# Both FFN products of a streaming-encoder layer by seven half-size products

## The chip, the cores and the metric

The kernel runs on one core of a Trainium2 chip. The metric is device time in microseconds, the median of several runs of the whole program. TensorE is written PE, VectorE DVE, ScalarE ACT, GpSimd POOL, SyncE SP; SP issues most transfers.

## The reference

One layer of a streaming encoder over 2048 prompt tokens and 64 sample tokens, 2112 in all, width 1024, in float32. Attention and a causal depthwise convolution feed an output projection; then come the FFN, a gated embedding and a final norm. What matters here is this:

```python
    mixed = jnp.concatenate([rms_norm(attn, lp['attn_out_g']), rms_norm(conv, lp['conv_out_g'])], axis=-1)
    x = x + mixed @ lp['w_out']
    f = rms_norm(x, lp['norm_ffn_g']) @ lp['w_ff_up']              # 1024 -> 4096
    x = x + jnp.square(jax.nn.relu(f)) @ lp['w_ff_down']           # 4096 -> 1024
    x = x + jax.nn.sigmoid(rms_norm(x, lp['norm_ple_g']) @ lp['w_ple_gate']) * (p @ lp['w_ple_proj'])
```

## The kernel before

The tokens stand in 17 tiles of 128 (the last has 64). Up to three tiles make a piece, two pieces a block, and there are three blocks (line 53), of 768, 640 and 704 tokens. Phase 1 projects the input, phase 2 is attention, phase 3 (`phase3`) takes the blocks one after the other through output projection, FFN, gated embedding and final norm.

Every float32 product is made of three matmuls, `mm3` (lines 177 to 181): both operands are split into a rounded high part (a cast on ACT) and the rest (a difference, on DVE unless another engine is named) by `split` (lines 163 to 165), and high by high, high by low and low by high are added up in PSUM.

The FFN walks through the 4096 hidden channels in eight chunks of four slices of 128. For each slice `up` (line 973) multiplies the 1024 x 128 weights with each of the two pieces, 24 matmuls over as many columns as the piece has tokens; ACT and DVE take max(0, x) squared from PSUM to SBUF, and the result is split. Then the down product multiplies the four slices with their 1024 columns of down weights; each token tile and half of the output has 12 matmuls of 512 columns, and DVE adds the bank to the tile's row of `x1` (lines 1058 to 1061). The last piece, whose tokens end in half a tile, is multiplied with the weights as the stationary operand instead and transposed at the end (`down_tall`, line 997). Nothing of the FFN leaves SBUF. The norm of the FFN's input is not applied to its operand: since relu squared is homogeneous, its square is multiplied in where the down product is added (`Y`, line 1060).

The operand of the up product is made by `operand` (lines 202 to 219), eight groups of transposes with their split: for one piece as soon as its output projection is done, while PE projects the other. In the same way `prepare` and `mixed` (lines 838 to 861) make the operand of the next block's output projection during the gate of the present one, in SBUF tiles of their own (`h`, three of them), so that loads of the next block do not wait for rows of this one.

Matmuls go round four PSUM banks (`mm`), transposes round three (`tr`), one bank is left to the convolution. The convolution of later pieces, 31 taps per channel and token on DVE in small steps, is background work: `pin` (line 167) queues so many steps behind an instruction of the FFN. A scheduler orders the instructions of each engine beforehand; on the chip each engine takes them in that order. It looks at priorities and free buffers, and the number of buffers of a name (`bufs`) says how far a producer can run ahead.

## Time and profile before

| | |
|---|---|
| median of three runs | 3080.7 us (3079.17 to 3084.36) |
| span of the profiled execution | 3076.4 us |
| PE busy | 2940.3 us, 96% |
| PE weight loads busy | 2604.4 us, 85% |
| DVE busy | 2047.9 us, 67% |
| ACT busy | 1215.2 us, 40% |
| POOL busy | 878.3 us, 29% |

The span goes from the first instruction to the last. The profiled execution's time is this span and what little lies around it; the median of the runs is 4.3 us above the span. Busy is the time in which an engine has an instruction under way. Matmuls are pipelined, so PE counts as busy even where the next matmul could have started earlier, and how fast it works is read from the distance between starts. Phase 3 begins at about 1130 us and takes the rest of the span.

### The profile page before, as it was taken

Reading aid. Unit: us, or ns where it says so; the run is one execution under the profiler, and the core shown is the slowest. Engines: PE = TensorE matmul, PEld = TensorE weight load, DVE = VectorE, ACT = ScalarE, POOL = GpSimd, SP = SyncE. Lnnn points to the kernel's source line nnn. Section 1 sums busy time; section 2 is a strip of 40 time slices with the busy share of each in tenths; the row PEclk is TensorE's granted clock in tenths of the full one; section 3 lists DMA queues with packets and bytes.
Section 4 is the critical chain, followed back from the end, with each engine's and each line's share of the span. In section 5 each row is a group of like instructions: output and inputs, shape, how many; then the busy total and the mean of one; then the engine's idle time right before and its main releaser. Section 6 shows DMA issues by size and latency. Waiting matters only on the chain.

```text
span 3076.4 us, 42553 instructions
## 1 busy us (share of the span) xinstructions
PE 2940.3 (96%) x15586; PEld 2604.4 (85%) x15586; DVE 2047.9 (67%) x3533; ACT 1215.2 (40%) x2404; POOL 878.3 (29%) x1498
## 2 busy tenths in 40 slices
PE   8998899989989879999999999999999999999998
PEld 7997888667667769999999888998998799999986
DVE  4489693999999866666665556787775544444453
ACT  6443342767666734222222433222234432321242
POOL 3235555877776730002002020003022100000001
PEclk9999999999998989999999999999999999999999
DMA  6635258743331132111222242232232411221121
GB/s 200 207 115 181 82 167 166 107 66 57 56 53 31 32 123 74 61 57 64 71 84 78 81 162 69 68 108 68 73 109 92 144 48 62 83 76 55 62 92 45
DMA packets 148601, 279.12 MB, mean 91 GB/s; under 512 B 38136, under 2 KB 78824, under 8 KB 146952
## 3 DMA queue, kind: packets, MB, share of 16 engines
q1 hardware_dynamic: 123800, 244.35, 24.7%
q0 software_dynamic: 24592, 32.06, 6.5%
q8 instruction: 122, 2.00, 0.3%
q14 instruction: 87, 0.71, 0.1%
HBM read 225.67 MB, written 51.28 MB: 90 GB/s over the span
## 4 chain that ended last, share of the span: by engine, by line
PE 72%; DVE 15%; DMA 4%; issue 4%; POOL 3%; ACT 1%; SPq 1%; DVEq 0%; POOLq 0%; ACTq 0%
PE mm L179 23%; PE mm L181 23%; PE mm L180 23%; DVE pl L754 6%; DVE mx L715 3%; DVE cacc L614 2%; PE tr L211 2%; PE tr L714 1%; PE acc L762 1%; DMA qr<-q_s 1%; DMA qr<-in_mq 1%; DMA h<-in_x 1%; POOL rt L153 0%; POOL ry L155 0%; DVE su L777 0%
## 5 line engine op out<-in xcount | busy, mean ns | idle before, releaser
L179 PE MATMUL mm<-thi,uh 128*128 128x384 f32 (+2 forms) x1488 | 480.8, 324 | 0.0
L180 PE MATMUL mm<-tlo,uh 128*128 128x384 f32 (+2 forms) x1488 | 480.7, 323 | 0.0
L181 PE MATMUL mm<-thi,ul 128*128 128x384 f32 (+2 forms) x1488 | 480.3, 323 | 0.0
L614 DVE SCALAR_TENSOR_TENSOR cacc<-cu,cw,cacc 128x384 f32<-128x384 f32 (+2 forms) x720 | 445.1, 632 | 7.3
L758 POOL TENSOR_TENSOR px<-px 128x512 f32<-128x512 f32 (+5 forms) x304 | 399.6, 1315 | 124.7 <-ACT px L753 65.4
L179 PE MATMUL mm<-wdh,ah 128*128 128x512 f32 x896 | 349.5, 391 | 4.9 <-DVE x L1060 2.9
L180 PE MATMUL mm<-wdl,ah 128*128 128x512 f32 x896 | 348.8, 390 | 0.0
L181 PE MATMUL mm<-wdh,al 128*128 128x512 f32 x896 | 345.2, 390 | 0.0
L983 ACT ACTIVATE rl<-mm 128x384 f32<-128x384 f32 (+1 forms) x192 | 88.1, 459 | 590.6 <-PE mm L181 590.2
L152 POOL TENSOR_TENSOR rt<-ry 128x3 f32<-128x3 f32 (+2 forms) x150 | 38.0, 254 | 987.0 <-DVE ry L149 980.2
L754 DVE TENSOR_TENSOR pl<-px,ph 128x512 fp32r<-128x512 f32 (+5 forms) x344 | 309.3, 913 | 15.2 <-ACT px L753 14.1
L1060 DVE SCALAR_TENSOR_TENSOR x<-mm,y,x 128x512 f32<-128x512 f32 x224 | 166.6, 749 | 206.9 <-PE mm L181 204.8
L180 PEld LDWEIGHTS mm<-tlo,uh 128*128 128x128 f32 x1488 | 280.2, 188 | 0.5
L179 PEld LDWEIGHTS mm<-thi,uh 128*128 128x128 f32 x1488 | 279.9, 188 | 0.7
L181 PEld LDWEIGHTS mm<-thi,ul 128*128 128x128 f32 x1488 | 280.1, 188 | 0.1
L165 DVE TENSOR_TENSOR wdl<-raw,wdh 128x1024 fp32r<-128x1024 f32 x139 | 170.8, 1230 | 116.7 <-ACT wdh L164 115.5
L752 ACT ACTIVATE ph<-mm 128x512 fp32r<-128x512 f32 (+5 forms) x344 | 179.3, 522 | 119.6 <-PE mm L181 102.4
L164 ACT CAST wdh<-raw 128x1024 fp32r<-128x1024 f32 x139 | 146.0, 1050 | 157.9 <-DMA raw<-in_wdn 87.1
L179 PEld LDWEIGHTS mm<-wdh,ah 128*128 128x128 f32 x896 | 168.3, 188 | 40.6 <-DVE x L1060 3.3
L181 PEld LDWEIGHTS mm<-wdh,al 128*128 128x128 f32 x896 | 168.2, 188 | 35.0
L180 PEld LDWEIGHTS mm<-wdl,ah 128*128 128x128 f32 x896 | 168.3, 188 | 33.7
L602 POOL DMA_DIRECT2D cu<-u_s x20 | 11.2, 558 | 637.9 <-DVE cacc L614 637.5
(297 smaller groups left out, 6854.4 us busy)
## 6 DMA issues: line engine op xcount, KB each, us to landing
raw<-in_wup SPq DMA_DIRECT2D x96, 512.0 KB, 3.2
raw<-in_wdn SPq DMA_DIRECT2D x96, 512.0 KB, 3.2
raw<-in_wglu SPq DMA_DIRECT2D x24, 512.0 KB, 4.6
raw<-in_wout SPq DMA_DIRECT2D x24, 512.0 KB, 4.5
raw<-in_wgate SPq DMA_DIRECT2D x24, 512.0 KB, 3.8
v_s<-vst SPq DMA_DIRECT2D x36, 256.0 KB, 2.8
v<-v_s POOLq DMA_DIRECT2D x8, 1152.0 KB, 9.2
h<-in_x SPq DMA_DIRECT2D x16, 512.0 KB, 4.5
```

Of the source, the lines that this page charges most:

```text
L164: self.nc.scalar.copy(out=hi, in_=raw)
L165: return (eng or self.nc.vector).tensor_tensor(out=lo, in0=raw, in1=hi.bitcast(F32), op=ALU.subtract)
L179: t.matmul(ps, sh, mh, start=start, stop=False)
L180: t.matmul(ps, sh, ml, start=False, stop=False)
L181: t.matmul(ps, sl, mh, start=False, stop=stop)
L614: nc.vector.scalar_tensor_tensor(out=a, in0=U[:, k:k + W], scalar=w, in1=a, op0=ALU.mult, op1=ALU.add)
L715: nc.vector.tensor_reduce(out=mx[:n, b:b + 1] if nb > 1 else top, in_=ps[:n, :w], axis=AX.X, op=ALU.max, negate=True)
L752: nc.scalar.activation(out=ph[b:, s], in_=ps[:, s], func=AF.Exp)
L754: nc.vector.tensor_tensor(out=pl[b:, s], in0=px[b:, s], in1=ph[b:, s].bitcast(F32), op=ALU.subtract)
L758: nc.gpsimd.tensor_tensor(out=rs[b:, s], in0=rs[b:, s], in1=px[b:, s], op=ALU.add)
L983: nc.scalar.activation(out=rl[:, :N], in_=ps[:, :N], func=AF.Relu)
L1060: r = nc.vector.scalar_tensor_tensor(out=x1[t][:n, cs], in0=ps[:n, :], scalar=Y[q][:n, j:j + 1], in1=x1[t][:n, cs], op0=ALU.mult, op1=ALU.add)
```

## The change

Both products of the FFN are made by one level of Strassen's multiplication in Winograd's form: each operand is cut into four quarters, seven products of quarters replace eight, and sums of quarters are formed before and after. Quarters of the weights are halves of the 4096 hidden channels by halves of the 1024 model channels, quarters of the activations are halves of the model (or hidden) channels by halves of a block's tokens. For this the blocks become 768, 768 and 576 tokens, halves of 384, 384 and 288; in the last block a half ends inside the tile of sample tokens.

- **Up operands.** When both pieces of a block are projected, `x1` is normalised, stored to DRAM (`x_s`) and scaled in place; transposed quarters go to `xf`, POOL forms four sums of them per group of channels (`winograd_right`), and seven operands `X[1]` to `X[7]` are split, in the SBUF that held the operands and weights of the output projection.
- **Up product**, 16 steps j of two slices of 128 hidden channels each. POOL forms four sums of the weight quarters (`winograd`); the seven weight quarters are split; each product has 12 matmuls. The order is 1, 2, 6, 5, 7, 4, 3; products 1, 6, 7 and 4 add up in one bank, 5 and 3 in another after 2 has left it, and in between ACT copies the bank's present content, so that each output is a copy plus a bank. Then relu squared, and POOL forms four sums of the four results; seven quarters of 128 x N are written to DRAM (`a_s`).
- In block 0 each step also forms four sums of the down weights on POOL and writes them to DRAM (`wt_s`), for all blocks.
- **Down product**, seven products of 16 steps: an activation quarter (192 KB, or 144 KB) and a 128 x 512 weight quarter (256 KB) are loaded and split (the activation's low part on POOL, the weight's on DVE), then nine matmuls of 512 columns into three banks (in the last block twelve of 288 into four); after each product the banks are added to one or two output quarters in `x1`, which is loaded again from DRAM.
- **Around it.** Rows of `x1`, the raw weights of the up product and the `h` of the next block now share six buffers (`x4`); `prepare` and `mixed` for the next block come behind `final` of the piece. Convolution steps are pinned two to an up step and two to five down steps.

The diff, cut to its core:

```diff
-BLOCKS = [[[0, 1, 2], [3, 4, 5]], [[6, 7, 8], [9, 10]], [[11, 12, 13], [14, 15, 16]]]
+BLOCKS = [[[0, 1, 2], [3, 4, 5]], [[6, 7, 8], [9, 10, 11]], [[12, 13], [14, 15, 16]]]
+PROD = [1, 2, 6, 5, 7, 3, 4]
...
+    def winograd(self, eng, x11, x12, x21, x22, new):
+        s1, s2, s3, s4 = new(), new(), new(), new()
+        eng.tensor_tensor(out=s1, in0=x21, in1=x22, op=ALU.add)
+        eng.tensor_tensor(out=s2, in0=s1, in1=x11, op=ALU.subtract)
+        eng.tensor_tensor(out=s3, in0=x11, in1=x21, op=ALU.subtract)
+        eng.tensor_tensor(out=s4, in0=x12, in1=s2, op=ALU.subtract)
+        return {1: x11, 2: x12, 3: s4, 4: x22, 5: s1, 6: s2, 7: s3}
+    def winograd_right(self, eng, x11, x12, x21, x22, new):
+        t1, t2, t3, t4 = new(), new(), new(), new()
+        eng.tensor_tensor(out=t1, in0=x12, in1=x11, op=ALU.subtract)
+        eng.tensor_tensor(out=t2, in0=x22, in1=t1, op=ALU.subtract)
+        eng.tensor_tensor(out=t3, in0=x22, in1=x12, op=ALU.subtract)
+        eng.tensor_tensor(out=t4, in0=x21, in1=t2, op=ALU.subtract)
+        return {1: x11, 2: x21, 3: x22, 4: t4, 5: t1, 6: t2, 7: t3}
...
+            def x4(name="x1"):
+                return pc_.tile([P, D], F32, name=name, tag="x1", bufs=6)
+            def r2(name="raw"):
+                return pc_.tile([P, 512], F32, name=name, tag="r2", bufs=6)
+            def w2():
+                return pc_.tile([P, 512], F32R, name="wh", bufs=10), pc_.tile([P, 512], F32R, name="wl", bufs=10)
+            def a15(dt=F32, name="a"):
+                return pc_.tile([P, 384], dt, name=name, tag="a15", bufs=13)
...
             def prepare(pi):
-                hs = [p.tile([P, D], F32, name="h", bufs=3) for _ in self.pieces[pi].tiles]
+                hs = [x4("h") for _ in self.pieces[pi].tiles]
...
+                        y = self.norms([x1[t] for t in pc.tiles], pc.tiles)
+                        for j, t in enumerate(pc.tiles):
+                            n = TILES[t][1]
+                            nc.sync.dma_start(out=x_s[t], in_=x1[t][:n, :])
+                            nc.vector.tensor_scalar(out=x1[t][:n, :], in0=x1[t][:n, :], scalar1=y[:n, j:j + 1],
+                                                    scalar2=None, op0=ALU.mult)
...
+                for k in range(4):
+                    a, b = left[k]
+                    c_, d_ = quad(k, 1), quad(k + 4, 1)
+                    T = self.winograd_right(nc.gpsimd, a, c_, b, d_, lambda: a15(name="xt")[:, :N])
+                    for i in (6, 5, 7, 3, 4):
+                        into(i, k, T[i])
...
+                for j in range(NJ):
+                    ra, rb = x4("ru"), x4("ru")
+                    nc.sync.dma_start(out=ra.rearrange("p (k c) -> p k c", k=KD), in_=I["wup"][j])
+                    nc.sync.dma_start(out=rb.rearrange("p (k c) -> p k c", k=KD), in_=I["wup"][j + NJ])
+                    S = self.winograd(nc.gpsimd, ra[:, :512], ra[:, 512:], rb[:, :512], rb[:, 512:], lambda: r2("s"))
...
+                    product(1, px, True)
+                    nc.scalar.copy(out=y11, in_=px[:, :N])
+                    product(2, py, True)
+                    nc.vector.tensor_tensor(out=y11, in0=py[:, :N], in1=y11, op=ALU.add)
+                    square(y11)
+                    product(6, px, False)
+                    nc.scalar.copy(out=y12, in_=px[:, :N])
+                    product(5, py, True)
+                    product(7, px, False)
+                    nc.scalar.copy(out=y22, in_=px[:, :N])
+                    nc.vector.tensor_tensor(out=y22, in0=py[:, :N], in1=y22, op=ALU.add)
+                    square(y22)
+                    product(4, px, False)
+                    nc.scalar.activation(out=y21, in_=px[:, :N], func=AF.Relu)
+                    product(3, py, False)
+                    nc.vector.tensor_tensor(out=y12, in0=py[:, :N], in1=y12, op=ALU.add)
+                    r = square(y12)
+                    A = self.winograd(nc.gpsimd, y11, y21, y12, y22, lambda: a15(name="as")[:, :N])
+                    for i in PROD:
+                        nc.sync.dma_start(out=a_s[i, j], in_=A[i])
...
+                    for j in range(NJ):
+                        ar = a15()[:, :N]
+                        nc.sync.dma_start(out=ar, in_=a_s[i, j])
+                        ah, al = a15(F32R, "ah")[:, :N], a15(F32R, "al")[:, :N]
+                        r = self.split(ar, ah, al, nc.gpsimd)
+                        wr = r2()
+                        if i in raw_of:
+                            f, h = raw_of[i]
+                            nc.sync.dma_start(out=wr, in_=I["wdn"][(f + j) * P:(f + j + 1) * P, h * 512:(h + 1) * 512])
+                        else:
+                            nc.sync.dma_start(out=wr, in_=wt_s[i, j])
+                        wh, wl = w2()
+                        r = self.split(wr, wh, wl)
+                        for b in range(nb):
+                            cs = slice(b * P, (b + 1) * P)
+                            if tall:
+                                self.mm3s(ps[b][:, :N], wh[:, cs], wl[:, cs], ah, al, fresh and j == 0, j == NJ - 1)
+                            else:
+                                self.mm3s(ps[b], ah[:, cs], al[:, cs], wh, wl, fresh and j == 0, j == NJ - 1)
...
                     if h == 1 and (bi < 2 or q == 0):
                         final(pc.tiles, x1, gfin)
+                    if h == 1 and bi < 2:
+                        M1 = mixed(2 * bi + 2 + q, prepare(2 * bi + 2 + q))
```

Where the change moves instructions, three places of the queues show it.

PE in the up product of block 0: before, at the border of two pieces (`mm` are PSUM banks, `uh`, `ul`, `wdh`, `wdl` weights, `thi`, `tlo` the operand).

```order
L181 MATMUL mm_13905<-thi_13654,wdl_13870 128x384
L179 MATMUL mm_13905<-thi_13654,wdh_13869 128x384
L180 MATMUL mm_13905<-tlo_13655,wdh_13869 128x384
L181 MATMUL mm_13905<-thi_13654,wdl_13870 128x384
L179 MATMUL mm_13951<-thi0_13499,uh_13945 128x384
L180 MATMUL mm_13951<-tlo0_13500,uh_13945 128x384
```

The same engine after, at the border of products 7 and 4 of a step (`T12`, `T13` are operand 7, `T6`, `T7` operand 4).

```order
L904 MATMUL mm_14240<-T13_13746,wh_14313 128x384
L905 MATMUL mm_14240<-T12_13745,wl_14314 128x384
L903 MATMUL mm_14240<-T6_13739,wh_14333 128x384
L904 MATMUL mm_14240<-T7_13740,wh_14333 128x384
L905 MATMUL mm_14240<-T6_13739,wl_14334 128x384
```

Before, the next 24 matmuls go to another bank; after, both products write the same bank, and the copy of the bank stands between them on ACT.

POOL ahead of block 0's FFN: before, the end of a norm, its square and the loads of the convolution.

```order
L154 TENSOR_SCALAR rt_13713<-rt_13713 128x3
L155 TENSOR_TENSOR ry_13712<-ry_13712,rt_13713 128x3
L969 TENSOR_TENSOR y2_13729<-ry_13712 128x3
L602 DMA cu_14632<-u_s1_70 128x30
L603 DMA cu_14632<-u_s2_71 128x384
```

POOL after, at the same place (`xt` are sums of activation quarters, `s` of weight quarters: L885 to L888 of the up weights, L894 to L897 of the down weights).

```order
L885 TENSOR_TENSOR s_14047<-ru_14044 128x512
L894 TENSOR_TENSOR xt_13823<-xf_13815,xf_13751 128x384
L886 TENSOR_TENSOR s_14048<-s_14047,ru_14043 128x512
L887 TENSOR_TENSOR s_14049<-ru_14043,ru_14044 128x512
L895 TENSOR_TENSOR xt_13824<-xf_13821,xt_13823 128x384
L896 TENSOR_TENSOR xt_13825<-xf_13821,xf_13815 128x384
L888 TENSOR_TENSOR s_14050<-ru_14043,s_14048 128x512
L894 TENSOR_TENSOR s_14204<-ru_14200 128x512
L897 TENSOR_TENSOR xt_13826<-xf_13757,xt_13824 128x384
```

The sums of the operand and those of two steps of weights stand mixed in one queue.

SP between block 0 and block 1: before, the attention rows of the next block are loaded ahead of this block's results.

```order
L847 DMA h_18570<-at_s9_102 128x512
L847 DMA h_18571<-at_s10_103 128x512
L847 DMA h_18570<-s_s3_78 128x512
L847 DMA h_18571<-s_s3_78 128x512
```

SP after: the results are stored first, from the buffers into which the attention rows are then loaded.

```order
L966 DMA out_y_p<-x1_16948 128x1024
L966 DMA out_y_p<-x1_16950 128x1024
L966 DMA out_y_p<-x1_16952 128x1024
L860 DMA h_20364<-at_s6_99 128x512
L860 DMA h_20364<-s_s2_77 128x512
```

The loads have moved behind the stores, and behind the final norm that the stores wait for.

## Rows read from the trace of the kernel before

**Rows 1.** Page, forty slices of the span: PE busy tenths, GB/s moved.

```profile
PE   8998899989989879999999999999999999999998
...
GB/s 200 207 115 181 82 167 166 107 66 57 56 53 31 32 123 74 61 57 64 71 84 78 81 162 69 68 108 68 73 109 92 144 48 62 83 76 55 62 92 45
```

**Rows 2.** Windows view, FFN: busy us of each engine (x instructions), PEclk, DMA share, GB/s.

```profile
1200.00:1250.00 50.00, 50.00 (x251) 45.05 (x251) 34.36 (x54) 9.15 (x16) 0.00 (x0) 1.00 0.13 43
```

**Rows 3.** Timeline, PE, FFN: start us, us, engine line op out<-in.

```profile
1215.07 0.34 PE L179 MATMUL mm<-thi,uh 128*128 128x384 f32 x1
...
1219.24 0.33 PE L179 MATMUL mm<-thi,uh 128*128 128x384 f32 x1
...
1226.12 0.39 PE L179 MATMUL mm<-wdh,ah 128*128 128x512 f32 x1
...
1245.84 0.39 PE L179 MATMUL mm<-wdh,ah 128*128 128x512 f32 x1
...
2530.06 0.31 PE L179 MATMUL mm<-ah,wdh 128*128 128x320 f32 x1
...
2535.78 0.31 PE L179 MATMUL mm<-ah,wdh 128*128 128x320 f32 x1
```

**Rows 4.** Timeline, attention, GpSimd and VectorE: start us, us, engine line op out<-in.

```profile
569.15 9.89 POOL L758 TENSOR_TENSOR px<-px 128x512 f32<-128x512 f32 x7
...
569.61 1.70 DVE L754 TENSOR_TENSOR pl<-px,ph 128x512 fp32r<-128x512 f32 x1
...
572.23 0.77 DVE L754 TENSOR_TENSOR pl<-px,ph 128x512 fp32r<-128x512 f32 x1
...
573.01 1.67 DVE L754 TENSOR_TENSOR pl<-px,ph 128x512 fp32r<-128x512 f32 x1
...
574.94 1.29 DVE L754 TENSOR_TENSOR pl<-px,ph 128x384 fp32r<-128x384 f32 x1
...
576.36 1.02 DVE L754 TENSOR_TENSOR pl<-px,ph 128x256 fp32r<-128x256 f32 x1
...
577.76 0.35 DVE L754 TENSOR_TENSOR pl<-px,ph 128x128 fp32r<-128x128 f32 x1
```

**Rows 5.** Groups by form, VectorE, 545 to 1050 us: count, busy us, mean ns.

```profile
L754 DVE TENSOR_TENSOR pl<-px,ph 128x512 fp32r<-128x512 f32 x203 | 229.7, 1141 | 12.1 <-ACT px L753 12.0
...
L754 DVE TENSOR_TENSOR pl<-px,ph 128x384 fp32r<-128x384 f32 x29 | 21.8, 750 | 0.0
```

**Rows 6.** Single lines: engine, operation, count, duration ns min/median/max, first and last start.

```profile
L165 DVE TENSOR_TENSOR al<-rl,ah x192: 408/551/1649, 1192.7 to 2946.4; 128x384 fp32r<-128x384 f32 x128, 128x256 fp32r<-128x256 f32 x32, 128x320 fp32r<-128x320 f32 x32
...
L165 DVE TENSOR_TENSOR wdl<-raw,wdh x139: 1161/1226/1491, 1095.7 to 3019.5; 128x1024 fp32r<-128x1024 f32 x139
...
L614 DVE SCALAR_TENSOR_TENSOR cacc<-cu,cw,cacc x720: 469/609/6760, 154.7 to 2261.0; 128x384 f32<-128x384 f32 x120, 128x256 f32<-128x256 f32 x30, 128x350 f32<-128x350 f32 x30
...
L983 ACT ACTIVATE rl<-mm x192: 370/482/494, 1190.7 to 2941.4; 128x384 f32<-128x384 f32 x128, 128x256 f32<-128x256 f32 x32, 128x320 f32<-128x320 f32 x32
...
L638 POOL TENSOR_TENSOR cs<-cs,lng x17: 1261/1294/1452, 314.5 to 2312.7; 128x512 f32<-128x512 f32 x16, 64x512 f32<-64x512 f32 x1
...
L567 POOL TENSOR_TENSOR cq<-cq,h x6: 1001/1016/1173, 111.6 to 456.8; 128x384 f32<-128x384 f32 x4, 128x256 f32<-128x256 f32 x1, 128x320 f32<-128x320 f32 x1
```

**Rows 7.** Timeline, into the third phase: start us, us, engine line op out<-in.

```profile
1115.13 1.47 SPq L847 DMA_DIRECT2D h<-at_s  x3
...
1120.57 1.95 DVE L850 TENSOR_TENSOR h<-h,ri 128x512 f32<-128x512 f32 x3 [2.75 <-DMA h<-at_s]
...
1123.56 0.17 DVE L146 TENSOR_SCALAR rv<-ss 128x3 f32<-128x3 f32 x1 [1.03 <-ACT junk L161]
...
1127.82 1.28 DVE L855 TENSOR_SCALAR h<-h,ry 128x512 f32<-128x512 f32 x3 [1.39 <-POOL ry L155]
...
1130.85 0.80 PE L179 MATMUL mm<-wdh,thi 128*128 128x512 f32 x1 [0.24 <-ACT thi L213]
```

375 lines of the change are left out of this document (187 added, 188 removed).

## The prediction

> **What bounds the kernel now.** I read the page's forty slices first. From the sixteenth on PE stands at nine tenths [rows 1]; this is the third phase (output projection, FFN, gated embedding), from about 1130 us. A window of it has PE busy throughout, at the full granted clock of 2.4 GHz, and GpSimd idle [rows 2]. So the time of this phase is the number of matmuls times their spacing. The mean duration of a matmul doesn't give that spacing, because matmuls overlap: a 384-column one lasts 0.33 us, but the next begins 0.17 us later. So I took starts from the timeline [rows 3]: 24 matmuls of 384 columns in 4.17 us are 0.1738 us each, 87 of 512 columns in 19.72 us are 0.2267 us, 39 of 320 columns in 5.72 us are 0.1467 us. The line through 320 and 384 gives 0.1331 us at 288 columns and 0.1196 us at 256. Then I read the attention phase, because it is the only place where VectorE and GpSimd are both loaded [rows 4, 5], the rows of the operations that the change multiplies [rows 6], and the hand-over into the third phase, where PE waits for a freshly prepared operand [rows 7].
>
> **What is removed.** Before, the up product takes 768 matmuls per piece: four pieces of 384 tokens, one of 320, one of 256: 3072 x 0.1738 + 768 x 0.1467 + 768 x 0.1196 = 738 us. The down product takes 192 matmuls of 512 columns for each of 14 token tiles and 768 of 320 columns: 609 + 113 = 722 us. After, each block makes 16 x 7 x 4 x 3 = 1344 up matmuls, of 384, 384 and 288 columns: 467 + 179 = 646 us; and down 1008 of 512 columns in the first two blocks and 1344 of 288 in the last: 457 + 179 = 636 us. 1460 - 1282 = **178 us less on PE**, all of it on the path. Output projection, gate and the first two phases keep their matmuls.
>
> **What is added in the up stage.** One of the 16 steps of a block holds 84 matmuls, 14.6 us (11.2 us in the last block). Product 4 adds to the bank that product 7 has just filled, after ScalarE has copied it; the order puts the two back to back with nothing between. The end of a matmul trails the next start by 0.16 us, the copy takes 0.48 us [rows 6], two signals I put at 0.1 us: 0.75 us, 48 times, 36 us. So PE needs 15.35 us a step, 11.95 in the last block.
> GpSimd: four weight sums of 512 columns at 1.29 and four activation sums of 384 at 1.02 us [rows 6] are 9.2 us; in block 0 four more of the down weights, 14.4 us; in the last block 8.4 us (0.81 us at 288 columns).
> VectorE: seven low parts of 512 columns at 0.69 us (between 0.551 at 384 and 1.226 at 1024 [rows 6]), three squares and, taken alike, four operations with a PSUM operand at 0.55, and 7.3 convolution taps that are pinned there, 0.61 us each in block 0 and 0.47 in block 1: 13.1, 12.1 and, with no taps, 8.0 us.
> Each alone fits under PE. Together they don't. While GpSimd ran seven sums without a gap (9.89 us, 1.41 each instead of 1.29), six VectorE differences with both inputs in SBUF took 6.80 us in place of 3.32 [rows 4]; over the whole attention phase the 512-column ones average 1.14 us in place of 0.69, the 384-column ones 0.75 in place of 0.55 [rows 5]. With those means VectorE needs 7 x 1.14 + 3 x 0.75 + 7.3 x 0.83 + 2.2 = 18.5 us a step in block 0, 17.1 in block 1, 11.6 in block 2. With the full stretch of rows 4 for the share of the step in which GpSimd is busy (T = 13.1 + 10.9 x 1.05 x 15.7/T and so on) it is 21.5, 18.0 and 12.7 us. I take 20, 17 and 12.2, as GpSimd is nearly as full in block 0 as in rows 4 and less in the others: 16 x (5.4 + 2.4 + 1.0) = **+140 us** over the bare matmuls, the 36 us included. Bounds: 42 us if VectorE hides all of it (GpSimd at 15.7 us stays a little above PE in block 0), 188 us with the full stretch.
>
> **What is added around it.** *Operands of the up product.* Before, they were made of one piece while PE projected the other. Now the seven operands need both halves, and PE's queue has the last transposes ahead of the first product. After the last projection a norm and its scaling come (from the first product of rows 7 to the scaled tile 7.3 us; I take 8), then on GpSimd 16 sums of 384 columns with eight weight sums of two steps between them, 16.3 + 10.3 = 26.6 us. PE has 48 matmuls of products 1 and 2 (8.3 us) and some 4 us of transposes to do: 22 us idle; 21 in the last block. Block 0 has seven more sums there, but they are work done ahead that the 20 us a step already count, so it is 22 again. **+66 us**, between 45 (half of the weight sums come earlier) and 105 (VectorE's 28 splits slow GpSimd).
> *From up to down.* GpSimd's queue holds the last four activation sums before the first low part of the down stage: add and square 1.1, four sums 4.1, a cast 0.5, a low part 1.0: 6.7 us, three times: **+20 us** (10 to 25).
> *Down stage.* A step is 9 matmuls, 2.04 us (12, 1.60 us, in the last block). VectorE: 0.69 + 1.1 taps x 0.61 + 0.26 of additions to x = 1.6 us alone, 2.3 with the means of rows 5, 3.44 by the stretch. GpSimd: 1.02 and some 0.4 of layer norms; ScalarE two casts, 1.1. Some of VectorE's excess goes into buffers: **+30 us** over the 224 steps of two blocks (0 to 90); the last block, without taps, nothing.
> *Between blocks.* The rows of the next block's attention now load into the buffers of x. From the issue of such a load to the first matmul on it 15.7 us pass [rows 7]; in front of it now stand the last gate tile's sum, a norm (4.3 us from its first step to the scaling), three 1024-column products (about 1.2 us each) and a write to DRAM that has to land: 13 us. Against 29 us PE has the gate of the second piece, 90 x 0.2267 = 20.4 us: 9 us idle; then the second piece's chain against 72 matmuls of projection (16.3 us): 4; slices of the operand 3. **+32 us** for two boundaries (15 to 50).
> *End of block 2.* The transposed sums go back through 40 transposes after the last product: **+8 us** (5 to 12).
> The loads and writes of the activations cost nothing as long as transfers keep up; the cover is the buffers that let a load start four steps early, and the price without it is the third rival.
>
> **Sum.** 140 + 66 + 20 + 30 + 32 + 8 = 296 us added, 178 removed: +118 us on the profiled span of 3076.4 us. The median of the runs lies 4.3 us above that span: 3076.4 + 4.3 + 118 = **3199 us**. All low ends: 117 added, 3020 us; all high ends: 470 added, 3373 us. Every gap of PE can also cost some slow-clock matmuls after it; I leave that inside the bounds.
>
> **Rivals.**
> *Faster: the additions hide.* VectorE gets its work in while GpSimd waits for data, the weight sums run ahead, and PE paces every stage except at the copies and hand-overs. For it: each engine alone is under PE's time, and in the FFN of before GpSimd is nearly unused. Against it: rows 4 and 5. Time by the low ends: 3020 us. It decides once all that is added stays under the 178 us removed: with the up stage at its 42, the other terms may come to 136 in place of my 156.
> *Strict exclusion.* What rows 4 show is a lock: of a GpSimd sum and a VectorE operation with two SBUF inputs only one runs, for its whole length. Then a step takes the sum of both: 14.4 + 10.9 = 25.3 us, 19.1 and 14.6: 297 us in place of 140; and the down stage 1.02 + 0.69 + 0.67 = 2.38 us, 76 us in place of 30: 3199 + 157 + 46 = 3402 us. For it: a difference begun beside a running sum took 1.70 us, its own 0.69 and most of a sum. Against it: in rows 4 the sums (9.0 us alone) and the differences (3.3 us) would need 12.3 us and took 9.9. The Trainium skill says this of the chip in "SBUF — State Buffer", section "Who interferes with whom": VectorE with two SBUF inputs and GpSimd reading SBUF share a port pair that is an exclusive lock. By that rule it is 3402 us; the trace agrees on who disturbs whom and bears out only part of the price.
> *Transfers bound.* A down step reads 459 kB in 2.04 us, 225 GB/s (410 kB in 1.60, 256 GB/s, in the last block); an up step of block 0 moves 4.5 MB. The busiest slice of the page shows 207 GB/s [rows 1]. Were that a ceiling, down steps would take 2.22 and 1.98 us, 82 us in place of 30, and block 0's steps 21.8 us, 29 more: 3280 us. For it: long single queue, rows of 1.2 to 2 kB. Against it: no slice looks limited by its transfers, as PE is full in slices of any rate.
>
> **How the numbers follow.** The forecast, between 3075 and 3373 us with 3199 as the middle: 0.48. Faster: 0.27, as the terms are many and the low end is below the old time. Strict exclusion 0.12, transfers 0.09. A sum within 0.2% of the old time, about what a measurement of this kernel can tell from no change: 0.04. Faster by over 0.2% is thus 0.27, within 0.04, slower 0.69. The range: the low end a little under the low sum, 3015; the high end short of the high sum, 3355, which leaves out strict exclusion and the best part of the faster case, some 0.18.
>
> **What would show it.** In the profile after: matmul spacing unchanged, 4032 + 3360 FFN matmuls in place of 4608 + 3456; PE gaps of about 0.75 us behind the copy of a bank, once a step; block 0's up stage longer than block 1's although both hold the same matmuls, with VectorE and GpSimd above nine tenths and 512-column differences above 1 us; gaps of some 20 us ahead of each up stage and of 9 and 4 us at block ends, at a lower granted clock. Wrong if up steps of block 0 take under 16.5 us, or if PE waits for DMA in the down stage. Both would show in PE's idle time by what ended it.

## The result and the profile after

The changed kernel takes 3672.9 us (median of four runs, 3672.0 to 3678.1) where the kernel before takes 3081.7 us; the ratio is 1.1925 (95% interval 1.1908 to 1.1942). The forecast was 3199 us with a range up to 3355 us: slower was right, but by 591 us and not by 118.

The page after, engines' busy time and three rows of the slices:

```profile
PE 3002.9 (82%) x14938; PEld 2509.3 (68%) x14938; DVE 2530.9 (69%) x3806; ACT 1517.4 (41%) x3172; POOL 1878.4 (51%) x2324
...
PE   8999888989888477777789867787888976888888
...
PEclk9999998999998799988999979998999988999999
...
GB/s 193 180 153 137 131 191 53 49 55 74 27 15 129 158 200 201 197 190 143 160 163 87 151 92 118 124 133 158 163 165 163 78 119 123 149 185 161 159 153 52
```

Up to the thirteenth slice the rows are like those of before [rows 1]; behind it the nines of PE have become sevens and eights. No other engine takes PE's place at nine tenths for long, and the transfers stay under 207 GB/s. Six windows, the middle of the three up stages and then of the three down stages (us, busy us of each engine with its instructions, PEclk, DMA share, GB/s):

```profile
1250.00:1580.00 330.00, 241.35 (x1179) 222.84 (x1179) 297.33 (x304) 83.06 (x156) 249.20 (x178) 0.92 0.61 203
2200.00:2480.00 280.00, 222.55 (x1160) 209.43 (x1160) 222.59 (x299) 81.13 (x153) 138.81 (x113) 0.96 0.37 123
3075.00:3270.00 195.00, 167.94 (x1176) 158.16 (x1176) 147.24 (x200) 78.48 (x156) 132.19 (x109) 0.99 0.47 151
1635.00:1915.00 280.00, 217.86 (x827) 153.68 (x826) 191.15 (x251) 105.74 (x196) 145.21 (x174) 0.95 0.50 156
2540.00:2805.00 265.00, 214.19 (x827) 151.73 (x826) 180.91 (x242) 103.86 (x195) 135.87 (x167) 0.97 0.52 163
3310.00:3540.00 230.00, 184.08 (x1069) 146.99 (x1070) 80.71 (x110) 87.82 (x180) 71.89 (x90) 1.00 0.53 161
```

The columns behind the length are PE, PEld, DVE, ACT and POOL. Only in block 0's up stage is VectorE near full (297 of 330 us). In the down stages no engine is: in the last one VectorE works 81 of 230 us, GpSimd 72, the transfers half of the time, and PE still waits. Before, a window of the FFN had PE busy for all of its 50 us [rows 2].

The stages, from PE's first and last matmul of each, against the bare matmuls at the spacing of before [rows 3]:

| stage | bare | forecast adds | measured | adds |
|---|---|---|---|---|
| up, with building X (from the last projection): 415.7 + 370.5 + 267.3 us | 646 | 140 + 66, and 12 of transposes | 1053.5 | 407 |
| last up product to first down product: 8.7 + 9.6 + 7.1 us | 0 | 20 | 25 | 25 |
| down: 345.2 + 327.6 + 283.1 us | 636 | 30 | 956 | 320 |
| block boundaries and end of block 2, by difference | | 32 + 8 | | 26 |

With the 178 us removed, that is the 600 us between the two profiled spans (3676.3 and 3076.4 us). The forecast added 296 us and lacks 482: three fifths of it (290) are in the down stage, two fifths (189) in the up stage. The 12 us of transposes were in the time of before as well, in another place; without them the last line is 38 us for the 40 forecast.

**Down stage.** Waits between 1600 and 1950 us, block 0's down stage and its edges (engine line <- releaser: us in all, times, longest):

```profile
POOL al L168 <- ACT ah L167: 130.1, 66, 5.9
ACT ah L167 <- DMA a<-a: 127.4, 76, 6.6
...
PEld mm L903 <- ACT ah L167: 85.2, 68, 4.9
```

PE waits for the cast of the activation (`ah`), and the cast waits for its load. The load itself takes 2.8 us from issue to landing (median), so the question is why it is issued so late. SP's queue in the same window:

```profile
SPq L1139 <- DVE wl L168: 130.5, 61, 4.4
SPq L1137 <- DVE wl L168: 83.2, 37, 6.0
...
SPq L1131 <- PE mm L905: 7.4, 2, 4.8
```

L1137 and L1139 load weights, L1131 loads the activation. The weight loads stand waiting for a free buffer, which VectorE's low part (`wl`) gives back; the activation loads hardly wait for anything of their own. They stand behind the weight loads in the queue. One passage of the timeline shows it (start us, us, engine line op, idle before):

```profile
1700.44 3.75 SPq L1139 DMA_DIRECT2D raw<-wt  x2
...
1703.16 0.68 DVE L168 TENSOR_TENSOR wl<-raw,wh 128x512 fp32r<-128x512 f32 x1
...
1704.30 1.13 SPq L1131 DMA_DIRECT2D a<-a  x2
1707.22 0.51 ACT L167 CAST ah<-a 128x384 fp32r<-128x384 f32 x1 [6.50 <-DMA a<-a]
...
1707.79 0.80 PE L903 MATMUL mm<-wh,ah 128*128 128x512 f32 x1 [3.95 <-ACT ah L167]
```

Two weight loads hold SP from 1700.44 to 1704.19; the second leaves when the low part that ends at 1703.84 has freed a buffer. Only then comes the activation load; its data is cast at 1707.22, and PE, idle for 3.95 us, starts at 1707.79. The order of the program says the same: the loads of the weights run ahead as far as their sixteen buffers (six raw, ten split) let them, so that activation n stands behind weight n+13. Here step 23 (`a_2_7`) is next to step 36 (`wt_4` of the third product):

```
L1131 DMA a<-a_2_7_13954 128x384
L1139 DMA raw<-wt_4_13101 128x512
```

With sixteen buffers, weight n+13 can only be loaded when PE is done with step n-3. So a loop goes round: PE's step n-3, cast and low part of a weight, weight load, activation load, cast, PE's step n. My estimate, from the durations above, is some 6 us besides a step's 2.04 us of matmuls (1.60 in the last block): about 8 us for three steps, 2.7 us each (2.5 in the last block), where 3.1, 2.9 and 2.5 us were measured (345, 328 and 283 us over 112 steps).

**Up stage.** Waits of PE in blocks 0, 1 and 2, 14 steps each:

```profile
PE mm L903 <- DVE y L1071: 53.4, 13, 9.9
...
PE mm L903 <- ACT y L1068: 28.5, 14, 15.7
```

```profile
PE mm L903 <- DVE y L1071: 31.3, 13, 2.6
...
PE mm L903 <- ACT y L1080: 13.4, 14, 1.0
PE mm L903 <- ACT y L1068: 12.4, 13, 1.0
```

```profile
PE mm L903 <- ACT y L1068: 24.4, 14, 12.5
...
PE mm L903 <- ACT y L1080: 13.0, 14, 0.9
...
PEld mm L903 <- DVE y L1086: 4.6, 14, 0.3
```

The forecast had one such wait a step (L1080, the copy between products 7 and 4). There are three: L1068, the copy of product 1 ahead of product 6; L1080 (14.2 us in block 0); and in blocks 0 and 1 L1071, the sum that must leave product 2's bank before product 5. In block 0 this sum is the longest. The timeline of block 2 shows what makes the copies late:

```profile
3117.09 0.62 ACT L167 CAST wh<-s 128x512 fp32r<-128x512 f32 x1 [1.02 <-PE mm L904]
...
3117.61 0.39 ACT L1068 COPY y<-mm 128x288 f32<-128x288 f32 x1
...
3118.06 0.40 PE L903 MATMUL mm<-T,wh 128*128 128x288 f32 x1 [0.92 <-ACT y L1068]
...
3122.78 0.29 PE L905 MATMUL mm<-T,wl 128*128 128x288 f32 x1
...
3123.03 0.62 ACT L167 CAST wh<-s 128x512 fp32r<-128x512 f32 x1 [1.01 <-PE mm L904]
...
3123.56 0.39 ACT L1080 COPY y<-mm 128x288 f32<-128x288 f32 x1
...
3124.00 0.40 PE L903 MATMUL mm<-T,wh 128*128 128x288 f32 x1 [0.93 <-ACT y L1080]
```

Ahead of each copy on ACT stands a cast of a weight that waits for a buffer (`wh`), and PE frees that buffer with the second-last matmul of the product whose end the copy follows, or of a later one. The cast goes first, 0.62 us, then the copy. From the last matmul's start to the next are 1.22 us instead of 0.13. Between the gaps the spacing is what it was: 35 steps from 3118.06 to 3122.78 are 0.135 us each, the first of them longer.

### The profile page after: what moved, and what is told of

Read it like the earlier page. It is cut to its first block, busy times and chain, and to the rows that moved or that the text cites. A ratio compares the mean times of both kernels' runs of the same rounds, so it can differ in the third digit from the quotient of the medians.

```text
span 3676.3 us, 47313 instructions
## 1 busy us (share of the span) xinstructions
PE 3002.9 (82%) x14938; PEld 2509.3 (68%) x14938; DVE 2530.9 (69%) x3806; ACT 1517.4 (41%) x3172; POOL 1878.4 (51%) x2324
## 5 line engine op out<-in xcount | busy, mean ns | idle before, releaser
L903 PE MATMUL mm<-T,wh 128*128 128x384 f32 (+1 forms) x1344 | 472.1, 351 | 251.9 <-DVE y L1071 96.8
L168 DVE TENSOR_TENSOR wl<-raw,wh 128x512 fp32r<-128x512 f32 x402 | 347.6, 871 | 405.5 <-ACT wh L167 395.0
L168 POOL TENSOR_TENSOR al<-a,ah 128x384 fp32r<-128x384 f32 (+1 forms) x336 | 337.7, 1008 | 461.3 <-ACT ah L167 425.3
L903 PEld LDWEIGHTS mm<-T,wh 128*128 128x128 f32 x1344 | 268.2, 200 | 298.9 <-DVE y L1071 106.5
L905 PE MATMUL mm<-T,wl 128*128 128x384 f32 (+1 forms) x1344 | 451.1, 336 | 4.8 <-DVE wl L168 4.8
L904 PE MATMUL mm<-T,wh 128*128 128x384 f32 (+1 forms) x1344 | 453.3, 337 | 0.9 <-DVE T L168 0.9
L903 PE MATMUL mm<-wh,ah 128*128 128x512 f32 x672 | 290.0, 432 | 110.6 <-ACT ah L167 109.5
L167 ACT CAST wh<-raw 128x512 fp32r<-128x512 f32 x402 | 245.7, 617 | 185.3 <-PE mm L905 87.4
L904 PE MATMUL mm<-wl,ah 128*128 128x512 f32 x672 | 274.9, 409 | 0.0
L905 PEld LDWEIGHTS mm<-T,wl 128*128 128x128 f32 x1344 | 267.3, 199 | 6.1 <-DVE wl L168 6.1
L904 PEld LDWEIGHTS mm<-T,wh 128*128 128x128 f32 x1344 | 268.6, 200 | 1.9 <-DVE T L168 1.7
L905 PE MATMUL mm<-wh,al 128*128 128x512 f32 x672 | 203.0, 411 | 14.8 <-POOL al L168 14.6
```

The source lines that it names most:

```text
L167: self.nc.scalar.copy(out=hi, in_=raw)
L168: return (eng or self.nc.vector).tensor_tensor(out=lo, in0=raw, in1=hi.bitcast(F32), op=ALU.subtract)
L903: t.matmul(ps, sh, mh, start=start, stop=False, skip_group_check=True)
L904: t.matmul(ps, sh, ml, start=False, stop=False, skip_group_check=True)
L905: t.matmul(ps, sl, mh, start=False, stop=stop, skip_group_check=True)
```

## The experiments

All kernels start from the changed one. The step of the up stage is the mean distance of the ReLU of product 4 from one step to the next, without the first and the last; the stages of the down product go from PE's first to its last matmul. The start of phase 3 itself moves by up to 11 us between executions (last projection of block 0 between 1193 and 1204 us), so stages are compared first, totals second. The kernels with a range were timed in four runs each; the others have one time.

| kernel | up step, us, blocks 0, 1, 2 | down stage, us, blocks 0, 1, 2 | time, us |
|---|---|---|---|
| changed | 22.8, 20.3, 13.8 | 345, 328, 283 | 3672.9 (3672.0 to 3678.1) |
| d_ring: own buffers for activations | 26.9, 23.5, 13.9 | 280, 272, 184 | 3594.0 (3585.6 to 3604.7) |
| d_hold: order of loads alone | 22.8, 20.3, 13.8 | 302, 290, 188 | 3499.8 |
| d_dve: low part on VectorE | 22.8, 20.3, 13.8 | 318, 312, 276 | 3624.0 |
| u_pipe: banks handed over behind other products | 23.9, 17.2, 12.1 | 341, 326, 287 | 3600.9 (3588.1 to 3604.8) |
| u_nosum: no sums of up weights | 21.0, 18.8, 13.7 | 341, 329, 287 | 3599.1 |
| u_nopin: no convolution in the up stage | 20.0, 17.1, 13.8 | 330, 323, 283 | 3590.1 |
| c_slot: u_pipe and own buffers | 23.9, 17.2, 12.1 | 281, 271, 183 | 3370.9 |
| x_defer: weight sums behind X | 23.7, 20.4, 13.8 | 342, 328, 290 | 3691.3 |
| x_dve: X's sums on VectorE | 23.0, 20.3, 13.8 | 341, 325, 289 | 3661.4 |
| x_nosum: X without sums | 22.8, 20.2, 13.8 | 346, 324, 283 | 3639.6 |
| c_best: c_slot, u_nopin, x_dve | 21.1, 14.7, 12.1 | 258, 255, 184 | 3312.6 (3307.8 to 3316.4) |
| c_nowt: c_best without sums of down weights | 17.7, 14.7, 12.1 | 258, 256, 184 | 3251.3 |

### d_ring: buffers of their own

```diff
-                return pc_.tile([P, 512], F32R, name="wh", bufs=10), pc_.tile([P, 512], F32R, name="wl", bufs=10)
+                return pc_.tile([P, 512], F32R, name="wh", bufs=8), pc_.tile([P, 512], F32R, name="wl", bufs=8)
...
-                        ar = a15()[:, :N]
+                        ar = pc_.tile([P, 384], F32, name="a", tag="ar", bufs=5)[:, :N]
```

> The same work in the down stage, but the loaded activation quarters have five buffers of their own, in place of a share in the thirteen, and the weights eight in place of ten. In the queue of SP the load of activation n then stands behind weight load n+2 at most, where it stood behind weight load n+13. Theory (queue): in the changed kernel the load of activation n cannot be issued before the weight load ahead of it finds a free buffer, which hangs on PE's step n-3; from there to the landed, cast activation some 6 us pass (cast 0.6, low part 0.9, issue 0.8, landing 2.8, cast 0.5), so a step takes (6 + 2)/3, about 2.9 us, measured 3.1, 2.9 and 2.5. With the new order the down steps fall to 2.1 to 2.4 us in blocks 0 and 1 and to 1.6 to 1.9 in block 2, the three down stages together from 956 us to about 700, and the whole to about 3420 us. Rival (GpSimd's low part, 1.1 to 1.4 us, and slow VectorE differences set the step): nothing changes by more than 50 us, over 3620 us. Rival (a ceiling of the transfers at 207 GB/s): down steps stay at 2.2 and 2.0 us or above, about 3440 us.

The down stages fell from 956 to 736 us. The total fell by 79 us only, to 3594 and not to the theory's 3420 (ratio to the kernel before 1.1666, 1.1637 to 1.1695): the up stage lost 4.1 and 3.2 us a step in blocks 0 and 1, which the expectation had not counted. I put that down to the smaller number of weight buffers; c_slot below, which keeps ten, loses nothing there against u_pipe. Three windows of its down stages:

```profile
1680.00:1900.00 220.00, 194.08 (x811) 152.43 (x810) 196.41 (x236) 95.54 (x186) 138.10 (x150) 0.98 0.61 190
2580.00:2800.00 220.00, 201.00 (x842) 157.06 (x841) 205.13 (x239) 96.55 (x189) 139.76 (x151) 0.98 0.62 195
3320.00:3470.00 150.00, 150.00 (x1141) 150.00 (x1140) 91.92 (x120) 90.40 (x191) 76.81 (x96) 1.00 0.87 260
```

In the last block PE never idles, at 260 GB/s: a ceiling of the transfers at 207 GB/s is out. In the first two VectorE is at 196 of 220 and 205 of 220 us, and a step takes 2.5 and 2.4 us. What is left there is (280 + 272) - 457 = 95 us, where I had taken 30, with an upper end of 90, for VectorE's excess. That VectorE makes these 95 us is not shown: no run takes work from it in this order of loads, and in the first window PE waits about as long for GpSimd's low part (`al`) as for VectorE's (`wl`); 14 of the 95 us are a gap at the start of the stage (see c_slot).

```profile
PE mm L905 <- POOL al L168: 13.5, 9, 2.8
PE mm L904 <- DVE wl L168: 12.2, 10, 2.7
```

### d_hold: the order on SP's queue alone

```diff
+                        with self.tc.issue_after(al_[n - 6].ins) if n >= 6 else ExitStack():
...
```

What is held is the weight load, which stays as it was; `al_` lists the activation loads.

> The changed kernel with one thing altered: weight load m of the down stage may stand in SP's queue no earlier than behind activation load m-6, so that activation load n stands behind weight load n+5, in place of n+13. Buffers and instructions are those of the changed kernel. Theory (queue): what the kernel with five own activation buffers gained came from the order on SP's queue alone; the three down stages fall from 956 us to about 740 us (2.4 to 2.5 us a step in blocks 0 and 1, 1.65 to 1.75 in block 2), up stage unchanged, about 3460 us. Rival (the gain came from more buffers for the activations): down steps stay above 2.8 and 2.4 us, over 3600 us.

With buffers and instructions as in the changed kernel the down stages fell to 302, 290 and 188 us, 779 us in all (740 expected): 177 of the 220 us. So it is the order that costs. What is left to d_ring is again in SP's queue, block 0's down stage:

```profile
SPq L1131 <- PE mm L905: 113.0, 60, 7.2
SPq L1140 <- DVE wl L168: 29.4, 23, 3.9
```

Now the activation loads wait, for one of the thirteen shared buffers that PE holds; this is the limit that the forecast had named as the only one.

### d_dve: GpSimd out of the down stage

```diff
-                        r = self.split(ar, ah, al, nc.gpsimd)
+                        r = self.split(ar, ah, al)
```

> The low part of the activation in the down stage is made on VectorE in place of GpSimd; the order of loads is as in the changed kernel (activation n behind weight load n+13). Theory (queue): the step of the down stage stays at 2.8 to 3.3 us in blocks 0 and 1 and 2.4 to 2.6 in block 2, 3600 to 3760 us. Rival (GpSimd's slow low part and its contention with VectorE set the step): it falls under 2.5 us, about 3480 us.

The steps stay at 2.84, 2.78 and 2.46 us. GpSimd's slow low part is worth 50 us of the 320, not their cause.

### u_pipe: every hand-over behind another product

PE's order per step is 6, 5, 7, then 1 and 2 of the next step, then 4, 3; the casts of weights are held behind the copies that PE needs first.

```diff
+                    old = [r for m, r in kept if m <= count[0] - 11][-1:]
+                    with self.tc.issue_after(old[0].ins) if old else ExitStack():
+                        wh, wl = self.copy_split(S[i], *w2())
...
+                    with self.tc.issue_after(last[0].ins) if last else ExitStack():
...
```

The first block holds a weight's cast and low part behind the copy of eleven products before, the second the twelve matmuls of a product behind those of the product before.

> Down stage as in the changed kernel; in the up stage PE's order is 6, 5, 7 of step j, then 1, 2 of step j+1, then 4, 3 of step j, so that between any two products on one bank whose copy or sum stands between them at least one other product runs, and on ACT a weight cast never stands ahead of a copy that PE needs before the cast's buffer comes free. Theory (hand-overs of banks): in the changed kernel three of them stop PE in each step for about 0.9, 1.0 and 0.3 to 4 us. Then the up step falls from 13.9 to 11.4 to 11.8 us in block 2, from 20.5 to about 17 in block 1 and from 23.6 to about 21 in block 0 (VectorE is then the bound), 16 x 8.3 = 130 us less, about 3540 us. Rival (VectorE's and GpSimd's load alone sets the step): blocks 0 and 1 stay, block 2 gains at most 2.3 x 16 = 37 us, about 3636 us.

Block 1 went to 17.2 us as expected, block 2 to 12.1 (11.1 in its first three steps, then 12.4), block 0 gained nothing a step, and its whole up stage 5 us; so the total is 3601 and not 3540 us (ratio 1.1679, 1.1656 to 1.1703). Its three up stages:

```profile
1260.00:1590.00 330.00, 239.88 (x1188) 235.08 (x1187) 308.69 (x309) 82.85 (x155) 240.39 (x171) 0.84 0.60 204
2200.00:2440.00 240.00, 214.89 (x1190) 211.36 (x1189) 237.02 (x307) 82.62 (x155) 139.26 (x113) 0.98 0.45 152
3050.00:3180.00 130.00, 120.41 (x896) 118.11 (x895) 129.28 (x152) 58.62 (x116) 108.09 (x82) 1.00 0.55 175
```

VectorE is now busy 309 of 330, 237 of 240 and 129 of 130 us. In blocks 1 and 2, with the hand-overs behind other products, it is the bound, and its times are what the forecast had worked out (17 and 12.2 us); c_best, without the convolution, takes block 1 to 14.7 us. In block 0 PE still waits for VectorE, in other places:

```profile
PE mm L903 <- DVE y L1094: 54.7, 11, 6.8
...
PE acc L632 <- DVE cacc L622: 34.2, 3, 11.7
```

L1094 is the sum that must leave product 5's bank before product 3, L632 the transposes of the convolution's result, which PE now reaches before VectorE has done the taps: the three waits lie in the three steps of 35 to 38 us, while the others take 14.7 to 25. VectorE is not the only limit of block 0, as c_best shows. In the changed kernel the waits came on top: VectorE and PE were waiting for each other in turn, and neither was full.

### u_nosum and u_nopin: what lies in the 20.3 us of block 1

```diff
-                    S = self.winograd(nc.gpsimd, ra[:, :512], ra[:, 512:], rb[:, :512], rb[:, 512:], lambda: r2("s"))
+                    q4 = [ra[:, :512], ra[:, 512:], rb[:, :512], rb[:, 512:]]
+                    S = {1: q4[0], 2: q4[1], 3: q4[2], 4: q4[3], 5: q4[2], 6: q4[0], 7: q4[1]}
```

> Leaves out the four sums of up weights per step: plain quarters are multiplied in their place. GpSimd is left with the activation sums and, in block 0, the sums of down weights. Theory (hand-overs of banks stop PE, and contention with GpSimd stretches VectorE on top): block 2 stays at 13.7 to 13.9 us a step, where VectorE is not full; block 1 falls from 20.5 to about 17.5 as the 512-column differences go back towards 0.69 us; the building of X falls from 51 to about 35 us as no weight sums stand between; about 3550 us. Rival (contention alone makes the whole excess of the up stage): block 2 falls to about 12 us too and block 1 to 15.5, about 3490 us. Rival (no contention): nothing but the building of X changes, about 3630 us.

```diff
-                    self.pin(r, 2)
```

> The changed kernel without the convolution steps in the up stage; they come later, in the down stage and ahead of the gate, where VectorE then has some 60 us of them by itself in each of two blocks. Theory (hand-overs of banks stop PE for about 4 us a step whatever VectorE has to do): the up step stays at or above 18.7 us in both blocks, 18.7 to 20 us, where it was 22.8 and 20.3. Rival (VectorE's load alone sets the step, as the prediction had it): with 6.6 to 8 us less of it a step, VectorE is under PE's 15.4 us and both blocks fall to 15 to 16 us. The whole: 3650 to 3720 us by the first, 3600 by the second.

Without weight sums block 2 is unchanged, as the first theory said; block 1 goes to 18.8 us, every step alike, and not to that theory's 17.5 (VectorE's 512-column differences stayed at 0.80 us), and the total to 3599 and not 3550 us. Product 6 of step 0 began 7, 13 and 14 us sooner, where 16 were expected (the up stages with X are 380.6, 333.8 and 251.2 us against 415.7, 370.5 and 267.3). Without the convolution: 17.1 us in block 1, which neither theory had (18.7 or more; 15 to 16). Block 1's waits of PE without sums, and then without convolution (L1072, L1069, L1081 answer to L1071, L1068, L1080 of the changed kernel):

```profile
PE mm L903 <- DVE y L1072: 23.4, 14, 4.4
...
PE mm L903 <- ACT y L1069: 12.8, 14, 0.9
PE mm L903 <- ACT y L1081: 11.8, 13, 0.9
```

```profile
PE mm L903 <- ACT y L1080: 13.4, 14, 1.0
...
PE mm L903 <- ACT y L1068: 12.4, 13, 1.0
```

The wait for the sum L1071 is gone with the convolution steps that stand ahead of it on VectorE; the two waits for copies stay whatever VectorE and GpSimd have to do. So of block 1's step 14.6 us are matmuls and 2.5 us the rest that neither run removes, mostly the hand-overs through ACT (in block 2: 13.8 - 11.2 = 2.6 us). The other 3.2 us go with the convolution; half of them (1.5 us, 20.3 - 18.8) go with the sums of weights as well. No run leaves out both, so how the two share the 3.2 us is not shown. In block 0 the convolution is worth 2.8 us and the up weights' sums 1.8 us of 22.8.

### c_slot: both faults mended

```diff
-                        ar = a15()[:, :N]
+                        ar = self.slot((0, 1, 2, 3, 8, 9, 10, 11)[n % 8], (P, 384), F32)[:, :N]
```

This is laid over u_pipe; the loads go to SBUF that X held.

> The up stage with its banks handed over behind other products (as in the run of that alone), and in the down stage the loaded activations in eight buffers that lie where the operands X were; weights keep ten buffers. Activation load n stands behind weight load n+1 to n+2. Theory: the two faults are independent and their gains add up: up stages as in that run (401, 310, 230 us), down stages 280, 272, 184 us, about 3600 - 218 = 3380 us. Rival (VectorE is the bound of the whole FFN, and what one stage gains the other pays): over 3450 us.

3370.9 us, within 10 us of u_pipe less d_ring's gain in the down stage: the two faults are independent. The gap of 7 to 10 us ahead of the first down product shrank to 0.9 us, as in d_ring, but the rest of it only moved behind the first few matmuls: 7.3, 6.4 and 4.0 us, counted in the down stage from here on. Blocks 0 and 2:

```profile
1618.12 0.47 PE L632 MATMUL acc<-ident,cacc 128*128 128x128 f32 x1 [7.29 <-DVE cacc L622]
...
3093.41 0.61 PE L904 MATMUL mm<-al,wh 128*128 128x288 f32 x1 [3.95 <-POOL al L168]
```

In the last block PE waits for GpSimd's first low part, which stands behind four activation sums; in the first two for the convolution's transposes, with that low part close behind. In c_best, where no taps stand there, all three blocks wait for the low part (3.8, 4.9 and 3.9 us). So GpSimd's queue, the forecast's cause, is real; in the changed kernel another wait ended later, the load of the activation in block 2 and the convolution's transposes in blocks 0 and 1.

### x_defer, x_dve and x_nosum: the building of X

```diff
+                    with self.tc.issue_after(xlast.ins):
...
```

What is held are the four weight sums of a step; `xlast` is the last sum of X.

> The changed kernel, but GpSimd makes no weight sum of the up stage before the last sum of the activation quarters. From the last projection to the first product that needs X complete (product 6 of step 0) the changed kernel takes 52.8, 50.8 and 37.3 us. Theory (GpSimd's queue: 16 activation sums of 1.35 us with 15 to 17 weight sums of 1.6 us between them make this time): the 16 sums take 22 us, two weight sums follow, and the time falls to about 37, 36 and 29 us; some of it is paid back in the first steps; about 3673 - 30 = 3640 us. Rival (VectorE's 28 splits set it): no change, 3670 us.

```diff
-                    T = self.winograd_right(nc.gpsimd, a, c_, b, d_, lambda: a15(name="xt")[:, :N])
+                    T = self.winograd_right(nc.vector, a, c_, b, d_, lambda: a15(name="xt")[:, :N])
```

> The changed kernel with the 16 sums of activation quarters per block on VectorE in place of GpSimd. Putting the weight sums behind them had made no net difference. Theory (GpSimd's whole queue of some 32 sums of 1.3 to 1.6 us makes the time until X is complete): from the last projection to product 6 of step 0 it falls from 52.8, 50.8 and 37.3 us to about 38, 36 and 30 us, as a sum costs VectorE some 0.55 to 0.75 us; nothing else changes, about 3635 us. Rival (VectorE's 28 splits and the weights' low parts are as long a chain): no gain or a loss, 3670 to 3690 us.

```diff
-                    T = self.winograd_right(nc.gpsimd, a, c_, b, d_, lambda: a15(name="xt")[:, :N])
+                    T = {6: a, 5: c_, 7: b, 3: d_, 4: d_}
```

> Leaves out the 16 sums of activation quarters per block: operands 3 to 7 of X are made of plain quarters, with the same casts and low parts. Measured from the last projection to the first ReLU of product 4 (step 0), the changed kernel takes 66.1, 63.8 and 62.7 us in the three blocks. Theory (GpSimd's queue makes this time): 16 sums of 1.35 us go, about 45, 42 and 45 us, and 3610 us in all. Rival (VectorE's 28 low parts with those of the weights make it): at most 10 us less in each, 3645 us or more.

From the last projection to the end of the up stage, the three blocks take 415.7, 370.5 and 267.3 us in the changed kernel; with the weight sums later 421.2, 370.5 and 265.9; with X's sums on VectorE 408.7, 362.7 and 266.9; without them 401.9, 356.7 and 255.1. The first is a miss (3691 us, not 3640): product 6 of step 0 did begin at 36.6, 36.6 and 38.2 us, as the theory had it for GpSimd's queue, but the first ReLU of product 4 came only 6 to 9 us sooner, and the first steps gave it all back. (In the changed kernel product 6 begins at 52.8, 50.8 and 52.5 us; the 37.3 in two of the expectations belongs to an earlier matmul.) The other two lie between their theories. The sums of X cost some 13 us a block, and moving them to VectorE, which in the changed kernel is already busy 44 of the 51 us there (block 1; GpSimd 42), returns half of that in two blocks and nothing in the last. What makes the rest is not settled; no single engine does.

### c_best and c_nowt: what is left

c_best joins c_slot, u_nopin and x_dve, with no edit of its own.

> All together: banks handed over behind other products, activation loads in buffers of their own, no convolution steps in the up stage, sums of activation quarters for X on VectorE. Theory (hand-overs and VectorE's load are both out of the way, PE or nearly PE sets the up stage): block 1's up step at 14.7 to 15.2 us, block 0's at 15.5 to 17.5 (GpSimd has 12 sums there), block 2's at 12.1 as before; down stages unchanged at 281, 271 and 183 us; some 18 us more of convolution ahead of each gate: about 3170 us, not faster than the kernel before. Rival (VectorE stays the bound through contention with GpSimd): block 0 stays over 20 us and block 1 over 16.5, over 3250 us.

```diff
-                        T = self.winograd_right(nc.gpsimd, ra[:, :512], ra[:, 512:], rb[:, :512], rb[:, 512:],
-                                                lambda: r2("s"))
+                        T = {4: ra[:, :512], 5: ra[:, 512:], 6: rb[:, :512], 7: rb[:, 512:]}
```

> The combined kernel without the sums of down weights: in block 0 the same four 512-column pieces per step are written to DRAM, but plain quarters in place of sums. In the combined kernel block 0's up step takes 20.3 us while block 1's takes 14.7, with GpSimd busy 195 of 240 us and 40 us more of it waiting until a written sum's buffer is free. Theory (GpSimd's twelve sums a step are the bound of block 0): 14.7 to 15.5 us a step, about 3312 - 85 = 3227 us. Rival (the transfers, 221 GB/s there, are the bound): stays above 18.5 us, over 3280 us.

c_best takes 3312.6 us, 1.0743 of the kernel before (1.0725 to 1.0761): 360 us less than the changed kernel and still slower than before; the theory had 3170 us. The down stages of blocks 0 and 1, expected unchanged, fell to 258 and 255 us; the wait for the convolution's transposes at their start is gone, the rest is open. Its windows of the up stage, blocks 0 and 1:

```profile
1300.00:1540.00 240.00, 193.32 (x974) 189.49 (x973) 142.69 (x160) 65.10 (x124) 195.03 (x140) 0.89 0.64 221
2130.00:2330.00 200.00, 200.00 (x1148) 200.00 (x1147) 129.25 (x200) 79.56 (x149) 136.11 (x101) 1.00 0.56 183
```

Block 1 is where the forecast wanted every block: PE full at 2.4 GHz, 14.7 us a step, 0.175 us a matmul. Block 0 stays at 20 to 21 us, the rival's value. There VectorE is no longer full, and PE's wait has moved:

```profile
ACT y L1088 <- POOL as L888: 59.5, 12, 6.3
...
PE mm L903 <- ACT y L1088: 46.7, 12, 5.3
POOL s L885 <- DMA wt<-s: 39.5, 11, 5.3
```

PE waits for a copy on ACT, which waits for a buffer that GpSimd's sum frees; and GpSimd waits besides until a sum is written to DRAM. Without the sums of down weights the step falls to 17.7 us, between the two theories: GpSimd's sums are worth 2.6 to 3.4 us of the 6 and more. In that kernel SP's queue has other waits (writes that stand behind loads), so what bounds the rest there stays open.

## Why the prediction failed, point by point

**The removal was right.** The spacing is unchanged; c_best's block 1 and the down stage of block 2 in d_ring (184 us, 0.137 us a matmul) run at it. 178 us did leave PE.

**Down stage, 30 us forecast, 320 measured: the step that failed first.** It is the sentence that "the loads and writes of the activations cost nothing as long as transfers keep up; the cover is the buffers that let a load start four steps early". The buffers were there and the transfers kept up, but the loads did not start: in the one queue of SP they stood behind weight loads that were waiting for their own buffers, and a step took 2.5 to 3.1 us instead of 1.6 to 2.04. The price that I gave for losing the cover, the third rival, was for the rate and not for the order (82 us). I had named "if PE waits for DMA in the down stage" as the sign of being wrong, and the sign is in the waits. The order could be read before the run: activation n stands behind weight n+13, sixteen buffers deep. I had counted the steps by which a load may run ahead, and not which load stands in front of it. d_hold shows 177 us of it by that order alone, d_ring and c_slot 220 us. Of the 100 us left, 95 are in blocks 0 and 1, 14 of them the gap at the start; so some 80 us stand against the 30 that I took for VectorE's excess (upper end 90), and how much of them is VectorE's and how much GpSimd's low part is open.

**Up stage and X, 218 us forecast (with the transposes), 407 measured.** Three parts:
- *Hand-overs.* "Product 4 adds to the bank that product 7 has just filled" is right, with 0.93 us of wait for my 0.75. But I put it under VectorE's time instead of adding it, and I missed the others: the scheduler runs products 1 and 2 of the next step early and leaves the copy of product 1 on ACT behind a cast that waits for a buffer, so product 6 waits as well; in blocks 0 and 1 the sum L1071 behind convolution steps makes a third. Together 2.5 us a step in block 2 and 4.2 in block 1, and more in block 0. u_pipe moves them behind other products and gains 3.1 us (block 1), 1.7 us (block 2) and nothing in block 0.
- *VectorE beside GpSimd.* The means of [rows 5] were the right size: in u_pipe VectorE is full at 17.2 and 12.1 us where I had taken 17 and 12.2. For block 0 I took 20; in u_pipe it is 23.9, more than the full stretch's 21.5, with PE's waits for L1094 and L632 in it and PE at 0.84 of its clock.
- *X.* 22 us of idle time a block against some 40: from the last projection to the copy that lets product 6 begin 52.3, 50.3 and 52.1 us pass, of which 8.3 us (6.4 in the last block) are matmuls and 4 us the transposes as I had put them. The term that was too small is GpSimd's queue: I had 16 sums of 1.02 us and eight weight sums of 1.29 us, 26.6 us; in block 1 GpSimd works 42 us before product 6 begins, with 15 sums of 1.34 us and 11 weight sums of 1.82 us on average, and x_defer shows that with fewer weight sums ahead of it product 6 begins sooner. For the time of the whole stage X's sums account for 13 us a block, the rest is open.

**Small terms.** Up to down 25 us for 20; GpSimd's queue is part of it, behind loads and convolution that I had not put there. Boundaries and end 38 us for 40, with the transposes as above; from a down stage to the next block's last projection PE is idle 15.3 and 14.8 us, where I had 16 each.

**The rivals.** Strict exclusion asked for 19.1 and 14.6 us a step in blocks 1 and 2. In u_pipe, with VectorE full and GpSimd busy 139 of 240 and 108 of 130 us, the steps are 17.2 and 12.1. So the two engines disturb each other, but a sum and a difference don't exclude each other for their whole length. The rule of the Trainium skill in "SBUF — State Buffer", section "Who interferes with whom", which calls the shared port pair an exclusive lock, names the right two engines; the trace agrees with it on who slows whom (block 1's squares on VectorE took 0.80 us beside the weight sums and 0.55 us without them), and differs on the price (17.2 us for 19.1, 12.1 for 14.6). Transfers as a bound are refuted by 260 GB/s in d_ring's last down stage.

**The signs.** Block 0's up step longer than block 1's: yes (22.8 and 20.3). VectorE and GpSimd above nine tenths there: VectorE just (297 of 330 us), GpSimd not (249). Differences of 512 columns above 1 us: yes in block 0 (1.16 us on sums and 1.01 on raw weights), not in block 1 (0.70 and 0.94). Gaps of 0.75 us once a step: three, mostly 0.9 to 2.6 us, in block 0 up to 9.9. Gaps of 9 and 4 us at block ends: about 5 and 5 at the first, 6 and 4 at the second.

## What to carry to other kernels

Work out for each load not only how many buffers let it run ahead, but what stands in front of it in its queue and on whom that waits: a load that runs far ahead and waits for buffers blocks the near one behind it, and the same holds for a cast that waits ahead of a copy. Waits between engines in series add to the busiest engine's time; they hide under it only if the order gives PE something else to do meanwhile. Fewer matmuls are worth having only where the engines that make the operands have the time: here 178 us off PE cost more than that even with the orders mended.

## What was unexpected about the hardware

The loads of a down stage went on at 260 GB/s for 150 us with rows of about 1 to 2 kB from a single queue (d_ring, block 2; 0.87 of the DMA engines' time), above every slice of the page before. In block 1 the squares on VectorE, both inputs in SBUF, took 0.80 us in the changed kernel and 0.55 us when GpSimd made no weight sums; the 512-column low parts did not change (0.80 us on average in both, 2200 to 2480 us and 2190 to 2440 us).
